# Transposes of a batch's cached keys: eight blocks in one step of the instruction order instead of four, and other pauses between steps

## Chip, cores and metric

The kernel runs on one core of a Trainium2 chip (trn2). The metric is the device time of one execution in microseconds. Three runs of the kernel before stand beside one profiled execution.

## What is computed

One step of a hybrid decoder layer for 256 prompt tokens and 32 sample tokens (8 batches of 4). Each sample batch has 256 cached keys and values, in two pages of a paged cache. The part that matters here is the attention of the sample tokens over the cached keys, in two branches: `x = 0` is stick-breaking attention, `x = 1` is block-sparse softmax attention, which with 256 cached keys comes to plain softmax over all of them.

```python
h = jnp.einsum('btd,de->bte', rms_norm(x, g), w_in)          # q, k, v of both branches, two gates
past_sbk = cache_sb_k[layer, page_table].reshape(dec_b, past_len, N_HEADS_SB, HEAD_DIM)
o_sb = stick_breaking(q_sb, jnp.concatenate([past_sbk, k_sb], axis=1),
                      jnp.concatenate([past_sbv, v_sb], axis=1), pos_s, k_pos_s)
m = sigmoid(gate_sb) * (o_sb @ w_proj_sb) + sigmoid(gate_mb) * (o_mb @ w_proj_moba)
x = x + m @ w_out
x = x + HierMoE(RMSNorm(x))
```

(The last three lines are shortened to their meaning.) The outputs are the normed results and the new keys and values.

## The kernel before

The work goes through four stages. First the input projection: 40 blocks of 128 output columns, each 24 matmuls of 128 x 288 (weights split into a high and a low part, `held`, lines 342 to 353; the tiles are called `g`). Into this dense stream the attention of the prompt and of the samples is woven. Then the two branch projections (tiles `p`), the output projection (tiles `o`), and last the experts, whose 50 MB of weights stream through a ring of buffers.

The order of TensorE's instructions is written by the kernel itself: line 136 puts PE under manual order, so PE gets its instructions as the Python code emits them. The class `Driver` (lines 78 to 119) decides that. It keeps a virtual clock `now` in nanoseconds. A stream (a generator such as `prompt_attn`, line 539, or `sample_attn`, line 601) emits a step and yields two numbers, a cost and a pause: the cost is added to `now`, and the stream is not asked again until the pause has also passed. While no stream is due, the dense stream emits its next pair of matmuls (cost 247). These numbers set the order alone; they are not times of the chip. The order on the other engines is made by a list scheduler when the program is built, so it can change when PE's order changes.

`sample_attn` works on groups `G` of four batches. For each batch it gathers the cached keys of one branch into a tile `kp` (POOL's indirect DMA, `pages`, line 593, into one of five buffers with the tag `pg`), and then for each half `c` of the keys it transposes four 128 x 128 blocks on PE (line 616) into a PSUM tile `pk`, which ScalarE or VectorE copies into `KT` (line 617). After four batches come 32 score matmuls into `ss` (line 622), the softmax or its stick-breaking counterpart, the transposes `pas` (line 634), the value product `pos` (lines 643 and 647), a masked copy `om` (line 650) and a last product `pd` (line 655).

PSUM tiles come from a pool with tags (line 142): `at` has four buffers. Every transpose of attention takes one of the four (`pk`, `pas`, `pa`, `ntr`, `ntv`, `rt`), and so do the prompt's scores (`sc`, two at a time, lines 545 to 561), `pos` and `pd`. A buffer is free again when its last reader is done. For the scores of branch 0 that is the subtraction in `soft_sb` (line 520), after three activations on ScalarE (513 to 515) and on VectorE the sum (517) and the scan (518). For the scores of branch 1 it is the second exponential (line 531). `pad` (lines 491 and 498) is the VectorE product that takes a finished `g` out of PSUM; the transposes `ntr` and `ntv` (line 414) read it. `rt` (line 459) transposes rotated heads.

Of the kernel before, what the change touches and what calls it, by code (L numbers as in the profile page):

```python
# [121 lines left out]
def build(tc, I, O):  # L122
# [21 lines left out]
    def P(tag, name):  # L144
        return ps.tile([128, 512], F32, tag=tag, name=name, bufs=NBUF[tag])
# [15 lines left out]
    def cc(name):  # L161
        a, b = AT[name]
        return blob[:, a:b]
# [233 lines left out]
    def start_sample(x):  # L397

        if S[x]["left"] or (x == 1 and "through" not in S[0]):
            return  # L400
        Qb = at.tile([128, 4, NB, NH, NQ], F32, tag="Qb", name=f"Qb{x}")
        nc.gpsimd.memset(Qb, 0.0)
        for j in range(4):
            for s in range(2):
                nc.gpsimd.tensor_copy(Qb[64 * s:64 * s + 64, j, :, 2 * j + s, :],
                                      S[x]["qT"][64 * s:64 * s + 64, j, 256:NT].rearrange("p (b q) -> p b q", q=NQ))
        S[x]["Qb"] = Qb
        drv.spawn(sample_attn(x), (3904.0, 3300.0)[x])
# [101 lines left out]
    def soft_sb(sc, w, resets, name):  # L510

        t = at.tile([128, 384], F32, tag="t1", name=f"t1{name}", bufs=2)
        nc.scalar.activation(t[:, :w], sc, AF.Abs)
        nc.scalar.activation(t[:, :w], t[:, :w], AF.Exp, scale=-1.0)
        nc.scalar.activation(t[:, :w], t[:, :w], AF.Ln, bias=1.0)
        s = at.tile([128, 384], F32, tag="t2", name=f"t2{name}", bufs=5)
        V.scalar_tensor_tensor(s[:, :w], sc, 0.0, t[:, :w], op0=ALU.max, op1=ALU.add)
        V.tensor_tensor_scan(out=t[:, :w][:, ::-1], data0=resets[:, ::-1], data1=s[:, :w][:, ::-1],
                             initial=0.0, op0=ALU.mult, op1=ALU.add)
        V.tensor_sub(s[:, :w], sc, t[:, :w])  # L520
        nc.scalar.activation(s[:, :w], s[:, :w], AF.Exp)
        return s
# [3 lines left out]
    def soft_mx(sc, segs, name):  # L526
        s = at.tile([128, 384], F32, tag="t2", name=f"p{name}", bufs=5)
        m = at.tile([128, 4], F32, tag="m", name=f"m{name}", bufs=4)
        for i, (a, b) in enumerate(segs):
            V.tensor_reduce(m[:, i:i + 1], sc[:, a:b], axis=AX.X, op=ALU.max, negate=True)  # L530
            last_exp[name[0] == "s"] = nc.scalar.activation(s[:, a:b], sc[:, a:b], AF.Exp, bias=m[:, i:i + 1],
                                                            accum_out=m[:, 2 + i:3 + i])
        ns = len(segs)
        V.reciprocal(m[:, 2:2 + ns], m[:, 2:2 + ns])
        for i, (a, b) in enumerate(segs):
            V.tensor_scalar_mul(s[:, a:b], s[:, a:b], m[:, 2 + i:3 + i])
        return s
# [55 lines left out]
    def pages(src, b, name):  # L593

        t = at.tile([128, 1024], F32, tag="pg", name=name, bufs=5)
        nc.gpsimd.indirect_dma_start(out=t, out_offset=None, in_=src,
                                     in_offset=bass.IndirectOffsetOnAxis(ap=pidx[:, b:b + 1], axis=0),
                                     bounds_check=NPHYS * PAGE // 2 - 1, oob_is_err=False)
        return t.rearrange("p (c d) -> p c d", c=2)

    def sample_attn(x):
        ck, cv = (I["cache_sb_k"], I["cache_sb_v"]) if x == 0 else (I["cache_moba_k"], I["cache_moba_v"])
        kT, vn, Qb = S[x]["kT"], S[x]["vn"], S[x]["Qb"]
        for G in range(2):
            pt = P("ss", f"ss{x}{G}")
            KT = []
            for bb in range(4):
                b = 4 * G + bb
                kp = pages(ck, b, f"kp{x}{b}")
                kt = at.tile([128, 1040], F32, tag="KT", name=f"KT{x}{b}", bufs=4).rearrange("p (j t) -> p j t", j=4)  # L610
                nc.gpsimd.tensor_copy(kt[:, :, 256:260], kT[:, :, 256 + 4 * b:260 + 4 * b])
                for c in range(2):
                    pk = P("at", f"pk{x}{b}{c}")
                    pv = pk.rearrange("p (j t) -> p j t", j=4)
                    for j in range(4):
                        nc.tensor.transpose(pv[:, j, :], kp[:, c, j * 128:(j + 1) * 128], ident)  # L616
                    nc.any.tensor_copy(kt[:, :, c:256:2], pv)  # L617
                    yield 440.0, (1051.0, 438.0)[x]
                KT.append(kt)
            for j in range(4):  # L620
                for bb in range(4):
                    mm(pt[32 * bb:32 * bb + 32, 0:260], Qb[:, j, 4 * G + bb, :, :].rearrange("p h q -> p (h q)"),  # L622
                       KT[bb][:, j, :], start=(j == 0), stop=(j == 3))
            mm(pt[:, 256:260], identb, newmask[x], start=False, stop=True, skip_group_check=True)
            yield 1900.0, 0.0
            if x == 0:
                a = soft_sb(pt[:, 0:260], 260, ones[:, 0:260], f"s{x}{G}")
                yield 0.0, 5569.0
            else:
                a = soft_mx(pt, [(0, 260)], f"s{x}{G}")  # L630
                yield 0.0, 5768.0
            pa = P("at", f"pas{x}{G}")
            for c in range(2):
                nc.tensor.transpose(pa[:, c * 128:(c + 1) * 128], a[:, c:256:2], ident)
            own = at.tile([128, 8, 4], F32, tag="own", name=f"own{x}{G}", bufs=2)
            V.tensor_mul(own, a[:, None, 256:260].broadcast_to([128, 8, 4]), cc(f"own{G}")[:, :, None].broadcast_to([128, 8, 4]))
            nc.tensor.transpose(pa[0:32, 256:384], own.rearrange("p b c -> p (b c)"), ident)
            aT = a
            nc.any.tensor_copy(aT[:, 0:256], pa[:, 0:256])
            nc.any.tensor_copy(aT[0:32, 256:384], pa[0:32, 256:384])  # L640
            yield 330.0, (3564.0, 1623.0)[x]
            po = P("at", f"pos{x}{G}")
            mm(po, aT[0:32, 256:384], vn[0:32, 2, :], start=True, stop=False)
            vps = [pages(cv, 4 * G + bb, f"vp{x}{G}{bb}") for bb in range(4)]
            for c in range(2):
                for bb in range(4):
                    mm(po[32 * bb:32 * bb + 32, :], aT[:, c * 128 + 32 * bb:c * 128 + 32 * bb + 32], vps[bb][:, c, :],  # L647
                       start=False, stop=(c == 1))
            om = at.tile([128, 512], F32, tag="om", name=f"om{x}{G}")
            V.tensor_mul(om.rearrange("p (h d) -> p h d", d=HD), po.rearrange("p (h d) -> p h d", d=HD),  # L650
                         cc("mask8")[:, :, None].broadcast_to([128, 8, HD]))
            yield 2700.0, 3712.0
            pd = P("at", f"pd{x}{G}")
            for j in range(4):
                mm(pd[:, j * 16:(j + 1) * 16], om[:, j * 128:(j + 1) * 128], cc("sel"), start=True, stop=True)
            nc.any.tensor_copy(oT[x][:, :, 256 + 16 * G:272 + 16 * G],
                               pd[:, 0:64].rearrange("p (j t) -> p j t", j=4))
            yield 430.0, 0.0
        if x == 0:
            S[0]["through"] = True  # L660
            start_sample(1)
# [705 lines left out]
```

## Time and profile before

| what | value |
|---|---|
| median of three runs | 415.95 us |
| lowest and highest run | 412.25 us, 420.18 us |
| the profiled execution | 413.99 us |
| its span, first to last instruction | 412.2 us |
| TensorE busy | 393.2 us of the span (95%) |
| mean granted TensorE clock | 0.989 |

Around the span of the profiled execution lie 413.99 - 412.2 = 1.8 us. PE is TensorE, DVE VectorE, ACT ScalarE, POOL GpSimd, SP the engine that issues most DMAs. Matmuls are pipelined, so the row of one is longer than the distance to the next start; the distance of starts is what one costs. A number in brackets behind a row is the idle time before it and what ended it.

### The profile page before, as it was taken

The page shows a single profiled execution, that of the slowest core. Times are in us where ns is not written, and L with a number is a line of the kernel's source. Part 1 is how long each engine was busy: PE and PEld are TensorE (multiplying, and loading weights), DVE is VectorE, ACT ScalarE, POOL GpSimd, SP SyncE. Part 2 cuts the span into 40 slices and gives each one's busy share as a digit, 9 for nine tenths or more (in the row PEclk, how much of TensorE's full clock was granted, in tenths as well). Part 3 has the DMA queues.
Part 4 walks back from the last instruction along what each step waited for, and adds up shares of the span by engine and source line. Part 5 has one row for each costly group of instructions (what it writes and reads, how often), then busy time and mean ns, then how long its engine had stood idle before and what let it go on. Part 6 is the DMA issues. An engine that isn't in the chain of part 4 may idle for free.

```text
span 412.2 us, 7107 instructions
## 1 busy us (share of the span) xinstructions
PE 393.2 (95%) x2706; PEld 293.5 (71%) x2706; DVE 207.9 (50%) x435; ACT 179.6 (44%) x349; POOL 94.3 (23%) x127
## 2 busy tenths in 40 slices
PE   7899999999999999999999999998999999999990
PEld 4799988858987977997999999984543333333350
DVE  3964468556543647134647785244540111126874
ACT  4854358577653664674554446232001111112353
POOL 3730222105343320610000232331002222033011
PEclk9999999999999999999999999999899999999997
DMA  8998636635743963663899999939599999999903
GB/s 263 327 355 277 222 103 230 223 118 205 260 158 91 338 235 103 220 240 103 192 381 395 341 324 389 409 88 303 189 313 413 410 416 412 417 414 410 343 32 122
DMA packets 56777, 111.12 MB, mean 270 GB/s; under 512 B 7621, under 2 KB 36941, under 8 KB 54689
## 3 DMA queue, kind: packets, MB, share of 16 engines
q1 hardware_dynamic: 49312, 86.56, 59.6%
q0 software_dynamic: 7120, 23.95, 15.8%
q8 instruction: 23, 0.38, 0.4%
q10 hardware_dynamic: 304, 0.09, 0.1%
q14 instruction: 18, 0.14, 0.1%
HBM read 104.72 MB, written 7.43 MB: 272 GB/s over the span
## 4 chain that ended last, share of the span: by engine, by line
PE 69%; DMA 20%; ACT 3%; issue 2%; DVE 2%; POOL 1%; SPq 1%; DVEq 0%; POOLq 0%
DMA w<-in_w_expert_up 15%; PE g L347 10%; PE g L351 10%; PE g L348 10%; DMA w<-in_w_expert_down 6%; PE gu L1154 4%; PE pk L616 3%; PE p L347 2%; PE p L348 2%; PE p L351 2%; PE ss L622 2%; PE o L347 2%; PE pos L647 2%; PE pd L1202 2%; PE po L588 2%
## 5 line engine op out<-in xcount | busy, mean ns | idle before, releaser
L347 PE MATMUL g<-xTh,hi 128*128 128x288 f32 x312 | 90.7, 311 | 0.0
L348 PE MATMUL g<-xTl,hi 128*128 128x288 f32 x312 | 85.7, 296 | 0.0
L1154 PE MATMUL gu<-w,xeT 128*64 128x512 f32 x256 | 62.0, 612 | 1.1 <-DMA w<-in_w_expert_up 0.7
L347 PEld LDWEIGHTS g<-xTh,hi 128*128 128x128 f32 x312 | 58.7, 188 | 1.0 <-issue 0.9
L348 PEld LDWEIGHTS g<-xTl,hi 128*128 128x128 f32 x312 | 58.9, 189 | 0.0
L351 PE MATMUL g<-xTh,li 128*128 128x288 f32 x312 | 50.5, 300 | 0.0
L333 DVE TENSOR_TENSOR li<-rawi,hi 128x1024 fp32r<-128x1024 f32 x39 | 47.3, 1215 | 3.0 <-ACT hi L328 3.0
L328 ACT CAST hi<-rawi 128x1024 fp32r<-128x1024 f32 x39 | 40.8, 1049 | 15.2 <-PE g L348 15.1
L351 PEld LDWEIGHTS g<-xTh,li 128*128 128x128 f32 x312 | 43.8, 189 | 1.7 <-issue 1.7
L1154 PEld LDWEIGHTS gu<-w,xeT 128*64 128x64 f32 x256 | 18.7, 139 | 33.1 <-issue 31.4
L1202 PE MATMUL pd<-w,hT 128*64 128x512 f32 x128 | 29.2, 598 | 0.0
L993 DVE TENSOR_TENSOR xeT<-xe,gpk 128x512 f32<-128x512 f32 x16 | 10.4, 686 | 22.9 <-PE xe L991 22.9
L617 ACT COPY KT<-pk 128x512 f32<-128x512 f32 x30 | 18.6, 639 | 7.1 <-PE pk L616 6.7
L1172 DVE SCALAR_TENSOR_TENSOR h<-gu,rsl,h 128x256 f32<-128x256 f32 x8 | 3.9, 484 | 34.3 <-ACT h L1169 34.3
L973 POOL DMA_INDIRECT xe<-x_d,inv x7 | 7.3, 1041 | 56.7 <-DVE rsl L1141 26.2
L1169 ACT ACTIVATE h<-gu,rsl 128x256 f32<-128x256 f32 x8 | 3.8, 474 | 37.5 <-PE gu L1154 19.8
L1202 PEld LDWEIGHTS pd<-w,hT 128*64 128x64 f32 x128 | 8.6, 136 | 15.4 <-issue 13.7
L616 PE MATMUL pk<-blob,kp 128*128 128x128 f32 x128 | 19.4, 274 | 0.1
L505 DVE TENSOR_TENSOR gate<-g,rb 128x288 f32<-128x288 f32 x16 | 7.3, 457 | 21.3 <-PE g L351 21.1
L347 PE MATMUL p<-oTh,hp 128*128 128x288 f32 x64 | 17.5, 296 | 0.0
L348 PE MATMUL p<-oTl,hp 128*128 128x288 f32 x64 | 17.4, 294 | 0.0
L1212 ACT COPY y<-pd 128x512 f32<-128x512 f32 x10 | 5.9, 586 | 23.6 <-PE pd L1202 23.6
(301 smaller groups left out, 708.6 us busy)
## 6 DMA issues: line engine op xcount, KB each, us to landing
rawi<-in_w_in SPq DMA_DIRECT2D x19, 1024.0 KB
w<-in_w_expert_gate SPq DMA_DIRECT2D x32, 512.0 KB
w<-in_w_expert_up SPq DMA_DIRECT2D x32, 512.0 KB
w<-in_w_expert_down SPq DMA_DIRECT2D x16, 1024.0 KB
rawo<-in_w_out SPq DMA_DIRECT2D x4, 1024.0 KB
y_d<-y POOLq DMA_DIRECT2D x10, 256.0 KB, 9.6
rawp<-in_w_proj_sb SPq DMA_DIRECT2D x2, 1024.0 KB
rawp<-in_w_proj_moba SPq DMA_DIRECT2D x2, 1024.0 KB
```

The source lines that it names most:

```text
L328: nc.scalar.copy(h, src)
L333: V.tensor_sub(l, src, h.bitcast(F32))
L347: mm(o, h[:, k, :], mh[k], start=(k == 0), stop=False)
L348: mm(o, h[:, k, :], ml[k], start=False, stop=False)
L351: mm(o, l[:, k, :], mh[k], start=False, stop=(k == n - 1))
L588: mm(po[64 * s:64 * s + 64, 128 * c:256], vn[:, c, h * 64:(h + 1) * 64], aT[s][:, 256 * c:256 + 128 * c], start=(c == 0), stop=(c == 1))
L616: nc.tensor.transpose(pv[:, j, :], kp[:, c, j * 128:(j + 1) * 128], ident)
L617: nc.any.tensor_copy(kt[:, :, c:256:2], pv)
L622: mm(pt[32 * bb:32 * bb + 32, 0:260], Qb[:, j, 4 * G + bb, :, :].rearrange("p h q -> p (h q)"), KT[bb][:, j, :], start=(j == 0), stop=(j = ...
L993: i = V.tensor_mul(xeT[:, ks, :], pv, gpk[:, ks, None].broadcast_to([128, 4, 128]))
L1154: mm(pt[64 * i:64 * i + 64, :], xeTs[pr][:, k, 64 * i:64 * i + 64], W[pr, k // 4, i][:, :, k % 4, :], start=(k == 0), stop=(k == 7))
L1202: mm(pd[64 * i:64 * i + 64, :], hT[:, k, 64 * i:64 * i + 64], W[pr, 2, i][:, k, c * 512:(c + 1) * 512], start=(k == 0), stop=(k == 1))
```

## The change

The yield moves out of the loop over the halves of the keys. A step is now both halves of a batch's keys, eight blocks into two PSUM tiles one after the other. The cost of a step is 880 instead of twice 440. The pause is 1800 (branch 0) or 1100 (branch 1) behind eight blocks, where it was 1051 or 438 behind four.

```diff
                     for j in range(4):
                         nc.tensor.transpose(pv[:, j, :], kp[:, c, j * 128:(j + 1) * 128], ident)
                     nc.any.tensor_copy(kt[:, :, c:256:2], pv)
-                    yield 440.0, (1051.0, 438.0)[x]
+                yield 880.0, (1800.0, 1100.0)[x]
                 KT.append(kt)
```

A batch took 2 x (440 + 1051) = 2982 of the virtual clock in branch 0 and takes 880 + 1800 = 2680; in branch 1 it took 1756 and takes 1980. The number of instructions on every engine is the same.

TensorE in branch 0, first group of batches, around the transposes of the third and fourth batch's keys. `pk` are the key transposes, `g` the dense blocks, `ntr` and `rt` transposes of the other branch's new heads; a number behind a name is a buffer's own. Before:

```order
L348 MATMUL g_836<-xTl,hi_832 128x288
L616 MATMUL pk_839<-blob,kp_809 128x128 x4
L347 MATMUL g_836<-xTh,hi_832 128x288
L348 MATMUL g_836<-xTl,hi_832 128x288
L414 MATMUL ntr_847<-blob,pad_113 128x128 x3
L459 MATMUL rt_861<-blob,nr_755 128x128 x3
L347 MATMUL g_836<-xTh,hi_832 128x288
L348 MATMUL g_836<-xTl,hi_832 128x288
L616 MATMUL pk_874<-blob,kp_868 128x128 x4
```

The same transposes `ntr` of `pad_113` in the changed kernel:

```order
L348 MATMUL g_860<-xTl,hi_856 128x288
L414 MATMUL ntr_867<-blob,pad_113 128x128 x3
L459 MATMUL rt_881<-blob,nr_787 128x128 x3
L616 MATMUL pk_892<-blob,kp_886 128x128 x4
L616 MATMUL pk_898<-blob,kp_886 128x128 x4
L347 MATMUL g_860<-xTh,hi_856 128x288
```

Where four groups of transposes in a row of the order were parted by two dense matmuls each, `ntr`, `rt` and both halves of a batch's keys now follow each other.

VectorE at the product `pad_113` that `ntr` reads. `t_765` to `t_788` belong to the second pair of prompt scores. Before:

```order
L617 COPY KT_731<-pk_793 128x4x128
L517 SCALAR_TENSOR_TENSOR t_779<-sc_765,t_775 128x384
L518 SCALAR_TENSOR_TENSOR t_775<-rst_99,t_779 128x384
L498 TENSOR_TENSOR pad_113<-g_744,rb 128x288
L333 TENSOR_TENSOR li_1002<-rawi_998,hi_1000 128x1024
L520 TENSOR_TENSOR t_779<-sc_765,t_775 128x384
L517 SCALAR_TENSOR_TENSOR t_788<-sc_766,t_784 128x384
```

And in the changed kernel:

```order
L517 SCALAR_TENSOR_TENSOR t_769<-sc_755,t_765 128x384
L517 SCALAR_TENSOR_TENSOR t_778<-sc_756,t_774 128x384
L518 SCALAR_TENSOR_TENSOR t_765<-rst_99,t_769 128x384
L518 SCALAR_TENSOR_TENSOR t_774<-rst_99,t_778 128x384
L498 TENSOR_TENSOR pad_113<-g_750,rb 128x288
L333 TENSOR_TENSOR li_1002<-rawi_998,hi_1000 128x1024
L520 TENSOR_TENSOR t_769<-sc_755,t_765 128x384
```

The product stood behind one sum and one scan; now both sums and both scans of the pair stand ahead of it.

TensorE in branch 0 after the first group's scores: `pa` are the transposes of two prompt heads' weights, `pos` the product with cached values. Before:

```order
L555 MATMUL sc_1071<-bfc 128x128
L351 MATMUL g_1004<-xTh,li_1002 128x288 x2
L579 MATMUL pa_1100<-blob,t_779 128x128 x3
L579 MATMUL pa_1105<-blob,t_788 128x128 x3
L459 MATMUL rt_1110<-blob,nr_1018 128x128 x3
```

And in the changed kernel:

```order
L647 MATMUL pos_1098<-vp_1112,t2s_941 32x512
L579 MATMUL pa_1126<-blob,t_769 128x128 x3
L579 MATMUL pa_1131<-blob,t_778 128x128 x3
L459 MATMUL rt_1136<-blob,nr_1015 128x128 x3
L351 MATMUL g_1004<-xTh,li_1002 128x288 x2
```

The value product moved ahead of the two transposes `pa`; it stood some rows behind them.

## Rows read from the trace of the kernel before

**Rows 1.** Page, busy time by engine, and the chain that ended last

```profile
PE 393.2 (95%) x2706; PEld 293.5 (71%) x2706; DVE 207.9 (50%) x435; ACT 179.6 (44%) x349; POOL 94.3 (23%) x127
PE 69%; DMA 20%; ACT 3%; issue 2%; DVE 2%; POOL 1%; SPq 1%; DVEq 0%; POOLq 0%
```

**Rows 2.** Windows: us; busy PE, PEld, DVE, ACT, POOL; clock; DMA share; GB/s

```profile
50.00:100.00 50.00, 47.64 (x390) 39.95 (x389) 32.27 (x65) 33.61 (x68) 11.34 (x16) 1.00 0.52 176
100.00:150.00 50.00, 50.00 (x436) 43.60 (x436) 25.26 (x60) 29.05 (x64) 18.45 (x25) 1.00 0.66 223
150.00:200.00 50.00, 50.00 (x408) 41.92 (x401) 22.53 (x50) 28.16 (x62) 9.24 (x16) 1.00 0.51 168
...
267.00:277.00 10.00, 10.00 (x85) 9.71 (x84) 3.05 (x17) 2.91 (x9) 4.09 (x6) 1.00 0.28 99
...
287.00:297.00 10.00, 8.79 (x38) 4.14 (x37) 6.03 (x18) 0.00 (x0) 2.07 (x2) 0.83 0.54 185
```

**Rows 3.** Timeline of PE, 58 to 74 us: start, duration, engine, line, operation

```profile
58.50 0.60 PE L616 MATMUL pk<-blob,kp 128*128 128x128 f32 x4
58.86 0.38 PE L347 MATMUL g<-xTh,hi 128*128 128x288 f32 x1
59.07 0.29 PE L348 MATMUL g<-xTl,hi 128*128 128x288 f32 x1
59.20 0.30 PE L347 MATMUL g<-xTh,hi 128*128 128x288 f32 x1
...
61.13 0.92 PE L552 MATMUL sc<-kT,qT 64*128 64x128 f32 x6 [0.15 <-ACT nr L445]
...
62.46 0.66 PE L616 MATMUL pk<-blob,kp 128*128 128x128 f32 x4
...
67.45 0.52 PE L414 MATMUL ntr<-blob,pad 128*128 128x128 f32 x3 [0.54 <-DVE t L518]
...
74.11 0.49 PE L459 MATMUL rt<-blob,nr 128*128 128x128 f32 x3
```

**Rows 4.** Timeline of ACT, 59 to 68 us

```profile
59.14 0.63 ACT L617 COPY KT<-pk 128x512 f32<-128x512 f32 x1
...
62.44 0.53 ACT L521 ACTIVATE t<-t 128x384 f32<-128x384 f32 x1 [1.36 <-DVE t L520]
...
64.03 0.94 ACT L514 ACTIVATE t<-t 128x384 f32<-128x384 f32 x2
64.85 0.52 ACT L515 ACTIVATE t<-t 128x384 f32<-128x384 f32 x1
...
66.63 1.13 ACT L617 COPY KT<-pk 128x512 f32<-128x512 f32 x2
```

**Rows 5.** Timeline of DVE, 61 to 93 us

```profile
61.85 1.01 DVE L520 TENSOR_TENSOR t<-sc,t 128x384 f32<-128x384 f32 x2
...
66.00 0.96 DVE L518 TENSOR_TENSOR_SCAN t<-rst,t 128x384 f32<-128x384 f32 x1
66.87 0.43 DVE L498 TENSOR_TENSOR pad<-g,rb 128x288 f32<-128x288 f32 x1
...
88.47 1.02 DVE L517 SCALAR_TENSOR_TENSOR t<-sc,t 128x384 f32<-128x384 f32 x2 [0.88 <-ACT t L515]
89.41 0.95 DVE L518 TENSOR_TENSOR_SCAN t<-rst,t 128x384 f32<-128x384 f32 x1
...
92.80 0.69 DVE L650 TENSOR_TENSOR om<-pos,blob 128x512 f32<-128x512 f32 x1
```

**Rows 6.** Timeline of PE, 85 to 99 us

```profile
85.80 0.81 PE L579 MATMUL pa<-blob,t 128*128 128x128 f32 x6
87.27 0.55 PE L459 MATMUL rt<-blob,nr 128*128 128x128 f32 x3 [0.66 <-ACT t L581]
...
98.97 0.55 PE L414 MATMUL ntr<-blob,pad 128*128 128x128 f32 x3 [0.81 <-ACT oT L656]
```

**Rows 7.** Timeline of POOL, gather of keys for the second group

```profile
92.91 1.02 POOL L596 DMA_INDIRECT kp<-in_cache_sb_k,pidx  x1 [14.66 <-PE pos L647]
```

## Prediction

> **What bounds the kernel now.** I read the page first, then the stretches, then the timelines of PE, ACT and DVE around the transposes that move. TensorE is busy for 95% of the span, and it makes 69% of the chain that ended last [rows 1]. In the stretch with the cached keys (50 to 200 us) PE has no idle time to speak of but 2.4 us between 50 and 100 us, DVE and ACT are busy for about half of the time, and the DMA queues too [rows 2]. So what an edit is worth here is read on PE alone: the sum of its instructions' costs, which this change leaves, and the waits of an engine that takes its instructions in order. DMA does bind later, among the experts, but between 267 and 277 us its share falls to 0.28 [rows 2]: the transfers have run ahead there and stand still until PE goes on. So I take a delay of PE ahead of that point to reach the end at full price, though part of it may be lost in that slack.
>
> Three waits can be seen in the stretch, and all hang on the four PSUM buffers `at`. At 67.45 the transposes `ntr` wait for VectorE, which has a scan (518) and then the product `pad` ahead [rows 3, 5]. At 87.27 `rt` waits for ScalarE's copy of `pa` (581), and at 98.97 `ntr` waits for ScalarE's copy of `pd` (656) [rows 6]. The key transposes at 62.46 start behind the subtraction (520) that frees a buffer of the prompt's scores: it starts at 61.85, two of them take 1.01, and the first is over at about 62.36 [rows 3, 5].
>
> **The change part by part.** *Fewer alternations.* Four key transposes start at 58.50, the dense block follows at 58.86, its second matmul 0.21 us later, and from there on the distance is 0.13 [rows 3]. So four transposes between dense blocks cost 0.36 and 0.08, that is 0.44 us, or 0.11 each.  Eight in a row are then 0.88 us, the same as twice four. The 16 joined steps save nothing by themselves; the bounds I keep are -1.3 (all 16 save the 0.08) and 0.
>
> *Moved waits.* Here I walk through the new order with the durations of the rows, on the clock of the trace before. "Late" means PE stands.
>
> Place A, branch 0, first group (from 58.50). Both halves of the first batch's keys are done at 59.4, four dense matmuls at 60.0. The prompt's second scores then need the two buffers the keys just filled. ScalarE's first copy starts at 59.14 and takes 0.63 [rows 4]; a second one starts 0.57 later (1.13 for two), so it ends at about 60.35: 0.4 late. The scores take 1.07, to 61.5. All four buffers are now scores, so `ntr` stands until the first subtraction ends at 62.4: 0.9 late. Then `ntr` (0.33), keys (0.44), 0.15 for the copy of `ntr`, keys again: 63.95. Twelve dense matmuls, four, eight key transposes, four and six more bring PE to 68.45, where it meets `ntr` of `pad_113`. ScalarE starts at 62.44 with two exponentials and two activations 513 (1.6, as 62.44 to 64.03), then 514, a key copy, 514, a key copy (0.41 + 0.57 + 0.41 + 0.57) and two of 515 (0.41 apart): the first 515 ends at about 66.5, the second at 66.9 [rows 4]. VectorE does both sums from 66.55 (0.47 each), both scans (0.87 from start to start, the time from 66.00 to 66.87) and `pad` (0.43): ready at 69.7 [rows 5]. So 1.3 late, where before the `pad` stood behind one sum and one scan. Behind it `ntr` and `rt` fill the two free buffers, the next keys wait for the copy of `ntr`: 0.4 late. The fourth batch's keys are done at 71.7. Before, they were done at 74.11 [rows 3], with 26 dense matmuls (3.47) and one `ntr` (0.33) more behind them, that is 70.3 for the same work. Place A costs 1.4 us.
>
> Place B, branch 0, after the first group's scores. The value product now precedes `pa`. It holds one buffer until `om`, the scores hold two until 520, so both `pa` go through the last one: the second waits for the first one's copy (0.33 and about 0.35 behind the start: 0.65 late), and `rt` waits for `om`, which on VectorE stands behind two sums and one scan (from about 89.2: 0.94, 0.87, then `om` 0.69, to 91.7 [rows 5]) while PE is there at 91.0: 0.7 late. The 1.35 stand against the wait at 87.27 before: `pa` takes 0.66 of work from 85.80, so it was 0.8 [rows 6]. Place B costs 0.55.
>
> Place C, the second group's first keys. `pd` is copied by VectorE now, both halves follow without a wait, and `ntr` comes later: the wait of 0.81 before 98.97 [rows 6], 1.0 with the tail of the matmul ahead, goes. What is late next is `rt` behind the second batch's keys, which asks for a buffer of the scores and gets it when 520 ends. On my clock those scores end at 96.6 and the first 515 at 98.95; behind it VectorE has a sum, a scan, a sum, a `pad` and 520 (0.47 + 0.87 + 0.47 + 0.43 + 0.5 [rows 5]), to 101.75, and PE is there at 101.3: 0.5 late. Place C gains 0.5.
>
> Place D, branch 1. Two dense matmul groups between key halves go, and the scores of the second pair need the buffers of the first, free after the second exponential: about 0.2 late. The fourth batch's second copy ends just as the 32 score matmuls reach it: 0.15. PE was not idle from 100 to 200 us before [rows 2], so nothing can be gained here but hidden tails. I take 0.35, with -0.3 and 1.0 as the ends (the upper end being one wait of place A's size).
>
> *The gathers.* Each half uses the same tile `kp`, so no key is needed before its transposes' step. The second group's second batch is issued at 92.91 [rows 7] and in my walk is first read at about 100.5; a step is 0.3 us shorter in the order, so I cost it at nothing. If that cover failed, the keys would be late by the excess of a gather over 7.6 us, and the three behind it with them.
>
> The sum: 1.4 + 0.55 - 0.5 + 0.35 = 1.8 us slower. On the profiled execution that is 413.99 + 1.8 = 415.8 us. That execution lies 2 us under the median of the runs; the median plus 1.8 would be 417.7. I take 417.0, between the two and nearer to the median.
>
> **The rivals.** *R1, the waits go.* With all that was late in the trace before gone (idle 0.15, 0.54, 0.66 and 0.81 in brackets [rows 3, 6], and some 0.25 of a matmul's tail ahead of each, as at 98.97 and 87.27: 3.2 us) the kernel takes 413.99 - 3.2 = 410.8. For it: longer pauses give the copies time, and place C does lose its wait. Against it: at place A four buffers are scores in either order.
>
> *R2, nothing moves.* Waits change places and cancel: 414 to 416. For it: VectorE and ScalarE have half of their time free [rows 2], so a wait that I count twice may be one. Against it: the scans that stand ahead of `pad` are a fact of the order.
>
> *R3, every pair waits (the slower side).* Place: each of the 16 steps. A step now takes two of four `at` buffers at once, so its second half could always stand behind a copy. Price: at the size of the wait at 98.97, 0.81 us each, 13 us, so 427. It decides from 0.52 us a step on, where 16 steps make 8.3 us. Against it: in my walk the second half itself is late by no more than 0.2, because ScalarE copies in 0.57 and there is dense work ahead of most steps.
>
> *R4, the clock.* Granted clock is 1.00 from 50 to 200 us, though PE stood for 2.4 us, and 0.83 between 287 and 297 us, after PE stood for 1.2 of ten [rows 2]. If the waits and the longer runs of transposes brought that 0.83 into the four stretches of key transposes, each as long as the first (58.50 to 74.11 [rows 3], 15.6 us, 62 in all), they would take 62 x (1/0.83 - 1) = 12.7 us more: 413.99 + 1.8 + 12.7 = 428.5. Against it: at place A PE stood for longer than anywhere in the stretch before and the clock stayed at its upper level, 2.4 GHz. The Trainium skill ("TensorE: Matmul & The Clock Gate", Part 4: PE-mode transpose) says that transposes do not count as PE activity in the way that matmuls do, and its section "A second HAM failure mode: psum-queue depth-cycling" tells of a kernel whose clock swings since PE halts briefly for PSUM buffers. By that rule this change, which lengthens runs of transposes and adds such halts, is a risk. The trace of before speaks against it, with 1.00 in the stretches that hold all 128 key transposes [rows 2].
>
> **How the numbers follow.** A measurement of this kernel can tell about 2% (8.3 us) from no change; the three runs alone spread over 8 us. Chances: my forecast 0.44, R2 0.25, R1 0.20, R3 0.07, R4 0.04. The forecast, R1 and R2 lie within 2%. Slower by over 2% is R3 and most of R4, less what of R3 stops short of it: 0.08. Faster by over 2% would need more than twice the waits that exist, and only the spread of the runs could show it: 0.03. Within 2%: 0.89. The range goes from R1 (410.8, about 411.5 with the runs' median above the profile) to the forecast with the upper ends of place D (1.0 for 0.35) and a doubled place A (1.4), 417.7 + 2.1, and 3 us for the spread of a median: 423. Outside stay R3, R4 and the far side of R1.
>
> **What would show it.** Right: idle of PE between 50 and 100 us above the 2.4 of before; `ntr` near 68 us waiting over a microsecond for VectorE with both scans ahead of `pad`; the second `pa` and `rt` after the value product waiting one behind the other; no wait of `ntr` at the second group's first keys; granted clock 1.00 up to 267 us. Wrong: key transposes themselves as the waiting row in most of 16 steps (R3), a clock below 1.00 there (R4), or PE without idle time between 50 and 200 us (R1). If PE loses its 1.8 us but the end does not move, the step that a delay reaches the end at full price has failed.

## The result, and the profile of the changed kernel

The changed kernel takes 417.56 us (median of 20 executions, 413.87 to 420.33), the kernel before 415.29 us in the same set (20 executions): ratio 1.007, 95% interval 1.0048 to 1.0092. In a second set (experiment 5) the ratio was 1.0045 (1.001 to 1.0079). These ratios leave out executions that took over 1.5% longer than the fastest of the same kernel. The changed kernel is slower by 0.5 to 0.7 per cent, less than the 2% that a measurement tells from no change with ease. The profiled execution of the changed kernel took 415.58 us with a span of 413.7.

Two lines of the page, busy time by engine and the chain that ended last, answer to [rows 1]:

```profile
PE 393.6 (95%) x2706; PEld 292.3 (71%) x2706; DVE 207.7 (50%) x435; ACT 178.8 (43%) x349; POOL 94.5 (23%) x127
PE 68%; DMA 18%; DVE 5%; ACT 3%; issue 2%; POOL 1%; DVEq 0%; SPq 0%; POOLq 0%; ACTq 0%
```

No engine's work has changed; the chain has 5% of VectorE where it had 2%. The windows of the changed kernel (columns as in [rows 2]):

```profile
50.00:100.00 50.00, 47.15 (x384) 39.20 (x384) 29.56 (x62) 32.76 (x68) 13.86 (x17) 1.00 0.51 168
100.00:150.00 50.00, 49.31 (x422) 42.84 (x424) 27.24 (x65) 28.53 (x62) 16.13 (x24) 1.00 0.67 228
150.00:200.00 50.00, 49.97 (x415) 40.76 (x408) 21.89 (x48) 27.70 (x62) 9.46 (x16) 1.00 0.49 161
267.00:277.00 10.00, 10.00 (x82) 9.73 (x81) 1.70 (x4) 1.69 (x5) 4.16 (x6) 1.00 0.33 132
```

PE stands for 2.85 us between 50 and 100 us (2.36 before) and for 0.69 between 100 and 150 (0.00 before); from 150 to 200 us there is no difference, and the clock is 1.00 in all of it. Where it stands is in the view of the waits of PE, here from 50 to 218 us (who waits, for whom; us in total, times, longest):

```profile
PE ntr L414 <- DVE pad L498: 1.0, 1, 1.0
PE ntr L414 <- DVE t L520: 0.9, 1, 0.9
PE pa L579 <- ACT t L581: 0.6, 1, 0.6
PE pas L637 <- DVE own L636: 0.5, 1, 0.5
PE pk L616 <- ACT nr L445: 0.2, 1, 0.2
PE rt L459 <- DVE t L520: 0.2, 1, 0.2
```

Before, four rows of this kind stood there: 0.15, 0.54, 0.66 and 0.81 [rows 3, 6]. Now the timeline of PE where they lie, with the rows that answer to [rows 3, 6], and the first matmul of the projection `p`:

```profile
58.30 1.04 PE L616 MATMUL pk<-blob,kp 128*128 128x128 f32 x8
59.09 0.38 PE L347 MATMUL g<-xTh,hi 128*128 128x288 f32 x1
59.31 0.30 PE L348 MATMUL g<-xTl,hi 128*128 128x288 f32 x1
...
62.26 0.55 PE L414 MATMUL ntr<-blob,pad 128*128 128x128 f32 x3 [0.89 <-DVE t L520]
...
69.46 0.52 PE L414 MATMUL ntr<-blob,pad 128*128 128x128 f32 x3 [0.98 <-DVE pad L498]
...
70.55 1.09 PE L616 MATMUL pk<-blob,kp 128*128 128x128 f32 x8 [0.24 <-ACT nr L445]
71.39 0.38 PE L347 MATMUL g<-xTh,hi 128*128 128x288 f32 x1
...
89.51 0.55 PE L579 MATMUL pa<-blob,t 128*128 128x128 f32 x3
90.62 0.55 PE L579 MATMUL pa<-blob,t 128*128 128x128 f32 x3 [0.57 <-ACT t L581]
91.26 0.55 PE L459 MATMUL rt<-blob,nr 128*128 128x128 f32 x3
...
97.08 1.12 PE L616 MATMUL pk<-blob,kp 128*128 128x128 f32 x8
...
101.39 0.55 PE L459 MATMUL rt<-blob,nr 128*128 128x128 f32 x3 [0.19 <-DVE t L520]
...
119.55 0.28 PE L637 MATMUL pas<-blob,own 128*32 128x128 f32 x1 [0.50 <-DVE own L636]
...
218.14 0.30 PE L347 MATMUL p<-oTh,hp 128*128 128x288 f32 x1
```

The last of these rows in the trace of before:

```profile
216.44 0.30 PE L347 MATMUL p<-oTh,hp 128*128 128x288 f32 x1
```

And the timeline of DVE that the waits hang on, which answers to [rows 5]: at 67 us the two scans ahead of `pad`, at 90 us `om` between the two scans, at 97 us the copy of `pd`, at 118 us a product of 1.22 us ahead of `own`:

```profile
66.22 1.02 DVE L517 SCALAR_TENSOR_TENSOR t<-sc,t 128x384 f32<-128x384 f32 x2 [2.00 <-ACT t L515]
67.16 1.80 DVE L518 TENSOR_TENSOR_SCAN t<-rst,t 128x384 f32<-128x384 f32 x2
68.88 0.43 DVE L498 TENSOR_TENSOR pad<-g,rb 128x288 f32<-128x288 f32 x1
...
88.73 1.02 DVE L517 SCALAR_TENSOR_TENSOR t<-sc,t 128x384 f32<-128x384 f32 x2 [6.30 <-ACT t L515]
89.67 0.95 DVE L518 TENSOR_TENSOR_SCAN t<-rst,t 128x384 f32<-128x384 f32 x1
90.54 0.67 DVE L650 TENSOR_TENSOR om<-pos,blob 128x512 f32<-128x512 f32 x1
91.12 0.95 DVE L518 TENSOR_TENSOR_SCAN t<-rst,t 128x384 f32<-128x384 f32 x1
...
97.27 0.23 DVE L656 COPY oT<-pd 128x64 f32<-128x64 f32 x1 [1.79 <-PE pd L655]
...
118.17 1.22 DVE L333 TENSOR_TENSOR li<-rawi,hi 128x1024 fp32r<-128x1024 f32 x1
119.30 0.19 DVE L636 TENSOR_TENSOR own<-t2s,blob 128x32 f32<-128x32 f32 x1
```

**Two numbers for each kernel.** From the start of the first key transposes to the start of the first matmul of the projection `p` (L347), PE has the same work in every kernel of this study (1280 instructions of the same kinds), so this time shows what its waits cost. It was 216.44 - 58.50 = 157.9 us before and 218.14 - 58.30 = 159.8 after: 1.9 us lost. From there to the end of the span it was 195.8 and 195.6. These two, taken from the timelines and the spans, and the granted clock in the windows between 270 and 300 us, stand in this table for all profiled executions, with the ratio of each kernel to the kernel before in its own set:

| kernel | to `p`, us | `p` to end, us | clock under 1.00 in windows of 10 us, 270 to 300 | ratio (95%) |
|---|---|---|---|---|
| before | 157.9 | 195.8 | 0.83 | 1 |
| changed | 159.8 | 195.6 | 0.83 | 1.007 (1.0048 to 1.0092) |
| 1, branch 0 alone | 159.8 | 198.6 | 0.86, 0.79 | 1.0071 (1.0037 to 1.0105) |
| 2, branch 1 alone | 158.1 | 193.8 | none | 1.002 (0.9983 to 1.0057) |
| 3, joined, old pauses | 161.8 | 196.3 | 0.83 | 1.0199 (1.0156 to 1.0241) |
| 4, apart, new pauses | 158.3 | 193.6 | none | 1.0016 (0.9984 to 1.0048) |
| 5, changed again | 159.9 | 197.3 | 0.86, 0.80 | 1.0045 (1.001 to 1.0079) |
| 6, scan behind `pad` | 159.0 | 193.7 | none | 1.0019 (0.9996 to 1.0041) |
| 7, as 3, copy on DVE | 160.3 | 196.9 | 0.89, 0.77 | 1.0068 (1.003 to 1.0106) |
| 8, before, copy on DVE | 160.1 | 197.6 | 0.89, 0.77 | 1.0063 (1.0031 to 1.0095) |
| 9, first batch apart | 159.4 | 195.2 | 0.83 | 1.0098 (1.006 to 1.0136) |
| 10, before, repaired | 156.7 | 194.0 | none | 1.0002 (0.9957 to 1.0048) |
| 11, as 10, again | 156.6 | 198.5 | 0.83, 0.83 | 0.9991 (0.9953 to 1.003) |
| 12, as 10, `rt` later | 156.6 | 198.2 | 0.75, 0.74 | 0.9992 (0.9955 to 1.003) |

The ratios also carry the granted clock, which differs from execution to execution. An estimate at equal clock can be worked out from all executions of an experiment and of the kernel before in its set: a straight line of time against mean granted clock, with one constant for the changed code. The constants are 2.0 us (experiment 1), 0.4 (2), 0.8 (4), 2.1 (5), 1.1 (6), 2.3 (7) and 2.6 (9), and for the repaired kernels about -0.5 (10), -0.2 (11) and 0.1 (12), each with a standard error of 0.2 to 0.3. Experiments 3 (3.3, error 0.5) and 8 (0.9) lose time by a lower clock too, which such a constant leaves out.

### The profile page after: what moved, and what is told of

Same layout as the page of the kernel before. It is cut to its first block, busy times and chain, and to the rows that moved or that the text cites. A ratio compares the mean times of both kernels' runs of the same rounds, so it can differ in the third digit from the quotient of the medians.

```text
span 413.7 us, 7106 instructions
## 1 busy us (share of the span) xinstructions
PE 393.6 (95%) x2706; PEld 292.3 (71%) x2706; DVE 207.7 (50%) x435; ACT 178.8 (43%) x349; POOL 94.5 (23%) x127
## 4 chain that ended last, share of the span: by engine, by line
PE 68%; DMA 18%; DVE 5%; ACT 3%; issue 2%; POOL 1%; DVEq 0%; SPq 0%; POOLq 0%; ACTq 0%
DMA w<-in_w_expert_up 15%; PE g L347 10%; PE g L351 9%; PE g L348 9%; DMA w<-in_w_expert_down 4%; PE gu L1154 4%; PE pk L616 2%; PE p L347 2%; PE p L348 2%; PE p L351 2%; PE o L347 2%; PE xe L982 2%; PE ss L622 2%; PE pd L1202 2%; PE po L588 2%
## 5 line engine op out<-in xcount | busy, mean ns | idle before, releaser
L347 PE MATMUL g<-xTh,hi 128*128 128x288 f32 x312 | 89.1, 307 | 0.0
L1154 PE MATMUL gu<-w,xeT 128*64 128x512 f32 x256 | 60.3, 598 | 1.2 <-DMA w<-in_w_expert_up 0.9
L347 PEld LDWEIGHTS g<-xTh,hi 128*128 128x128 f32 x312 | 58.7, 188 | 1.6 <-issue 1.6
L347 PE MATMUL p<-oTh,hp 128*128 128x288 f32 x64 | 17.5, 296 | 0.0
L616 PE MATMUL pk<-blob,kp 128*128 128x128 f32 x128 | 17.0, 275 | 0.3 <-ACT nr L445 0.2
```

The lines of the kernel that those rows point to most:

```text
L347: mm(o, h[:, k, :], mh[k], start=(k == 0), stop=False)
L1154: mm(pt[64 * i:64 * i + 64, :], xeTs[pr][:, k, 64 * i:64 * i + 64], W[pr, k // 4, i][:, :, k % 4, :], start=(k == 0), stop=(k == 7))
```

## The experiments

**1 and 2: which branch.** The diff of each against the changed kernel, first branch 0 alone, then branch 1 alone:

```diff
-                yield 880.0, (1800.0, 1100.0)[x]
+                    if x == 1:
+                        yield 440.0, 438.0
+                if x == 0:
+                    yield 880.0, 1800.0
```

```diff
-                yield 880.0, (1800.0, 1100.0)[x]
+                    if x == 0:
+                        yield 440.0, 1051.0
+                if x == 1:
+                    yield 880.0, 1100.0
```

Expected of the first:

> The joined step with its new pause in branch 0 alone; branch 1 keeps two halves and the old pause. Theory T1 (the cost is waits of TensorE at single places of branch 0: ntr behind the first subtraction and behind the product pad, the second pa, and the product own): the whole loss is here, 1.9 us of PE up to the first matmul of the gated projection p (216.44 us before, 218.14 after), PE waits for pad 1.0, for 520 0.9, pa 0.6, own 0.5 as in the changed kernel, ratio to the kernel before about 1.005 to 1.007. Rival T2 (each of the 16 joined pairs pays 0.1 to 0.2 us for its buffers, in both branches alike): half of the loss, ratio about 1.0035, and 0.9 us of PE.

Expected of the second:

> The joined step with its new pause in branch 1 alone; branch 0 as before. Theory T1 (all of the loss is waits in branch 0): ratio 1.000 (0.999 to 1.001), the waits of before at 67, 87 and 99 us stand again, and no new one between 140 and 200 us. Rival T2 (each joined pair pays alike): ratio about 1.0035, 0.9 us more PE between 140 and 200 us. My forecast on record had 0.35 us here, that is 1.0008.

Branch 0 alone has the six waits of the changed kernel, to 0.1 us, its 159.8 us to `p`, and its ratio; branch 1 alone has the waits of before and 158.1 us. So the loss is in branch 0, and the eight joined steps of branch 1 cost 0.2 us together. T2, a price per joined pair, falls.

**3 and 4: joining or the pause.** Experiment 3 joins the halves and gives a batch the time of two old pauses; experiment 4 leaves them apart with half the new time each:

```diff
-                yield 880.0, (1800.0, 1100.0)[x]
+                yield 880.0, (2102.0, 876.0)[x]
```

```diff
-                yield 880.0, (1800.0, 1100.0)[x]
+                    yield 440.0, (900.0, 550.0)[x]
```

> The steps joined, but with the time of two old pauses (2102 and 876) behind each, so that a batch takes as long in the order as before. In this order pad of the third key projection stands on DVE ahead of the second sum and of both scans. Theory T1 (what costs is where the new pauses put ntr, pad and own among the scans): ntr near 68 us waits for pad by less than 0.3 us where the changed kernel has 0.98, the wait of ntr for the subtraction 520 near 62 us (0.9) stays, since both pairs of key buffers stand ahead of the second scores here too; ratio to the kernel before 1.000 to 1.004. Rival T3 (joining alone is the cost, whatever the pause): ratio 1.006 or more, and waits in front of the key transposes.

> The halves stay apart as before, with half of the new time each (900 and 550): the pause alone. Theory T1 (place by place): the second scores come ahead of the second pair of halves, so the wait of ntr for 520 near 62 us goes back to under 0.2; pad stands on DVE behind one scan, so ntr waits for it by about 0.5 as before (1.0 after); ratio to the kernel before 0.998 to 1.002. Rival T3 (joining is the cost): also 1.000. Rival T4 (the longer pause alone is the cost): 1.006 or more.

Experiment 4 came out as T1 had it in time, 158.3 us to `p` and a ratio of 1.0016, though its longest wait is one of 0.7 us for the copy of `pd`, and none is left for `pad`. Experiment 3 is a miss: 1.0199 where T1 had at most 1.004. That is 8.2 us, of which the profiled execution shows 3.9 on PE up to `p` (161.8). Its waits of PE, 50 to 218 us:

```profile
PE pk L616 <- ACT oT L656: 2.4, 1, 2.4
PE ntr L414 <- DVE t L520: 0.9, 1, 0.9
PE rt L459 <- ACT t L581: 0.7, 1, 0.7
PE pos L643 <- ACT ps L640: 0.3, 1, 0.3
```

The wait for `pad` is gone and the 0.9 for 520 stays, as expected; but at the second group's first keys the second half waits 2.4 us for ScalarE's copy of `pd`, which stands behind a cast of 1.04 us and the activations of the scores. And the clock falls behind that wait, as the windows of experiment 3 show (columns as in [rows 2]):

```profile
90.00:100.00 10.00, 7.63 (x65) 5.81 (x58) 4.28 (x10) 6.19 (x14) 4.21 (x5) 0.97 0.82 266
100.00:110.00 10.00, 10.00 (x72) 9.98 (x72) 7.57 (x19) 5.31 (x10) 3.25 (x3) 0.85 0.40 120
```

T3 had the size (1.006 or more), but its reason, a cost of joining wherever it is done, does not fit: the greatest part of what PE loses up to `p` is one wait at one of 16 steps. Experiment 7 takes that wait away.

**5: the changed kernel again**, for the granted clock of each execution.

> The changed kernel once more, beside the kernel before on the same chip, for the granted clock of each execution. Theory T1 (waits of TensorE alone): the six waits of the changed kernel return at the same places within 0.1 us, the mean clock over its runs is that of the kernel before (0.989), ratio 1.004. Theory T5 (the waits also bring the granted clock down in some executions, as in the 10 us behind the wait of 2.4 us of the kernel with joined steps and old pauses): the mean clock is lower by 0.002 to 0.004, ratio 1.006 to 1.009.

The six waits return to the tenth of a microsecond, with 159.9 us to `p`. Ratio 1.0045, 1.9 us of 414.3, which is what PE loses, and 2.1 us at equal clock: T1's waits alone account for the loss. The mean granted clock over all twelve executions is 0.9866, and 0.9883 for the kernel before on the same chip, 0.0017 lower, where T5 had 0.002 to 0.004. So T5 is not needed for the loss, but that these waits never lower the clock in any execution is not shown.

**6: one scan behind `pad`.** The order on PE stays, row for row:

```diff
-            V.tensor_mul(t[:, 0:NT], o, rb)
+            i = V.tensor_mul(t[:, 0:NT], o, rb)
+            if j == 1 and not isq:
+                with tc.issue_after(i.ins):
+                    scans.pop()()
...
+        if name == "03":
+            scans.append(rest)
+        else:
+            rest()
```

(Shortened; `rest` is the scan, the subtraction and the exponential of `soft_sb`. The added lines move those in this file down, so that 520 is 524 in the rows below, 579 is 590 and 636 is 647.)

> The changed kernel with one scan on DVE, that of the second head of the second pair, put behind pad of the third key projection; the order on PE is the same row for row. If the 1.0 us that ntr waits near 69 us is due to that scan, as place A of the forecast has it, the wait falls to 0.0 to 0.3, the first matmul of the projection p comes 0.7 to 1.0 us earlier against the first key transposes than in the changed kernel, and the ratio to the kernel before goes from 1.007 to about 1.005. If the wait is set by something else (the product's own input, a matmul's tail), it stays at 0.7 or more.

The row of `pad` is gone from the waits of PE, the other five stand:

```profile
PE ntr L414 <- DVE t L524: 0.9, 1, 0.9
PE pa L590 <- ACT t L592: 0.6, 1, 0.6
PE pas L648 <- DVE own L647: 0.5, 1, 0.5
PE pk L627 <- ACT nr L445: 0.2, 1, 0.2
PE rt L459 <- DVE t L524: 0.2, 1, 0.2
```

159.0 us to `p`, 0.8 less than the changed kernel: that wait was set by the second scan on DVE. The ratio goes from 1.0045 to 1.0019 on the same chip; the two intervals overlap, but at equal clock the loss falls from 2.1 to 1.1 us, so the price of the wait reaches the end.

**7 and 8: the copy of the first `pd` on VectorE**, in the kernel of experiment 3 and in the kernel before, with PE's order unchanged:

```diff
-            nc.any.tensor_copy(oT[x][:, :, 256 + 16 * G:272 + 16 * G],
+            (V if (x, G) == (0, 0) else nc.any).tensor_copy(oT[x][:, :, 256 + 16 * G:272 + 16 * G],
```

> The kernel with joined steps and the old pauses, whose second key transposes waited 2.4 us for ScalarE's copy of pd, with that one copy on VectorE; the order on PE is the same row for row. Theory T1 (each loss is one wait at one place): the 2.4 us go, less than 0.5 us for VectorE in their place, the granted clock between 100 and 110 us is 1.00 instead of 0.85, and the ratio falls from 1.020 to 1.003 to 1.008. Rival T3 (joining with these pauses is slow by itself): the ratio stays at 1.015 or more.

> The kernel before with the copy of the first pd on VectorE instead of ScalarE; the order on PE is the same row for row. If the wait of 0.8 us at 98.97 hangs on ScalarE's copy, it goes with about 0.2 us of a matmul's tail: PE 1.0 us less up to the first matmul of p, ratio 0.997. If it hangs on pd itself or on something that VectorE would meet too, the wait stays and the ratio is 1.000.

In experiment 7 the 2.4 us become 0.8 where under 0.5 was expected (and 0.5 at a later pair), the clock stays at 1.00 between 100 and 110 us, and 1.0199 becomes 1.0068, as T1 had it. Up to `p` the two profiled executions differ by 1.5 us (161.8 and 160.3): so much are that wait and the clock behind it worth there. The two ratios, from different sets, differ by 5.4 us. The executions of experiment 3 have a mean clock of 0.977, those of experiment 7 one of 0.983; where the clock fell in those that were not profiled, no trace shows. Of what is left to experiment 7, 0.9 us is the wait for 520 that the changed kernel has too.

Experiment 8 is a miss in the other direction. The order on DVE puts the copy behind a scan, a product of 1.20 us, a sum and a subtraction, to 100.90 us, and `ntr` now takes the buffer of the key transposes and waits longer. The first row of its waits, and its window behind it:

```profile
PE ntr L414 <- ACT KT L617: 1.5, 1, 1.5
```

```profile
100.00:110.00 10.00, 10.00 (x70) 9.98 (x70) 5.61 (x17) 5.64 (x10) 2.25 (x2) 0.83 0.49 155
```

So the same edit takes a wait of 2.4 us away in one order and makes one of 0.8 into 1.5 in another. Of the twelve executions of this kernel ten have a mean clock of 0.976 to 0.981, two 0.993 and 0.994.

**9: only the first batch apart.**

```diff
+                    if (x, G, bb) == (0, 0, 0):
+                        yield 440.0, 1051.0
+                if not ((x, G, bb) == (0, 0, 0)):
+                    yield 880.0, (1800.0, 1100.0)[x]
```

> The changed kernel, but the very first key batch of branch 0 in two halves with the old pause; the other 15 batches joined. Theory T1 (the waits of the first group come from that one pair, which fills the buffers ahead of the second scores): the wait of ntr for 520 near 62 us and the second scan ahead of pad go, and ntr waits for pad by about 0.5 near 67 us as in the kernel before. But in this order pd stands five matmuls behind the scores and right ahead of the second group's first key pair, as in the kernel with old pauses, so the same wait of 2.4 us for ScalarE's copy of pd is to come back near 98 us, and with it (theory T5) a granted clock below 1.00 between 100 and 110 us: ratio 1.008 to 1.014. Rival T2 (each joined pair pays): ratio 1.0065, no wait over 1.1 us.

The first half of the expectation held: no wait for 520 near 62 us, and `ntr` waits 0.5 for `pad` (at 100.75, however, not near 67, where none is left). So that one pair makes both waits of the first group. The wait for `pd` came back, but with 1.1 us (the cast on ScalarE runs 1 us earlier than in experiment 3), and the clock stayed at 1.00. The ratio of 1.0098 is in T1's range for a reason that T1 did not give: PE loses 1.4 us to `p` in the profiled execution, and the ratio says 4. At equal clock it is 2.6. What the other executions do there, no trace shows.

Taken together: the wait for 520 stands where the first pair is joined (the changed kernel, experiments 1 and 3) and not where its halves are apart (before, 2, 4 and 9). The second scan ahead of `pad` needs the joined pair and the new pause together, since 3, 4 and 9 do not have it.

**10, 11 and 12: the kernel before with its waits repaired.** The scan behind `pad` as in experiment 6 (name "02"), and

```diff
-        yield 330.0, 5271.0
+        yield 330.0, 5271.0 + (600.0 if (j, isq) == (3, 0) else 0.0)
```

with 1000 for 600 in experiment 12; experiment 11 is the kernel of experiment 10 once more. (This edit, too, moves the lines down by up to ten.)

> The kernel before with its own waits repaired: the scan that stands ahead of pad of the third key projection put behind it, and the transposes rt of the fourth projection 0.6 us later in the order, which puts two matmuls ahead of them at 87 us and six ahead of ntr at 99 us. Theory T1 (a wait of PE is lost at full price, and so is its removal won): ntr near 67 us waits 0.0 to 0.2 instead of 0.5, rt near 87 us 0.0 to 0.4 instead of 0.7, ntr near 99 us 0.0 to 0.2 instead of 0.8; from the first key transposes to the first matmul of p 156.0 to 156.9 us instead of 157.9; ratio to the kernel before 0.994 to 0.998. Rival T6 (what is taken from one place turns up at the next): the waits return elsewhere, ratio 0.999 to 1.002.

> The repaired kernel before once more, since its interval (0.9957 to 1.0048) holds both the gain that its trace shows on PE (1.3 us, ratio 0.997) and none. Theory T1 (the gain reaches the end): ratio 0.994 to 0.999 in this set too, 156.7 us from the first key transposes to the first matmul of p. Rival T6 (the gain is given back behind p, in the experts): ratio 0.999 to 1.004 again, and from p to the end more than 194 us where no stretch of the trace has a clock below 1.00.

> As the repaired kernel, with the transposes rt of the fourth projection 1.0 us later in the order instead of 0.6, which puts four matmuls ahead of them at 87 us instead of two; the other places of the order on PE stay. Theory T1: the 0.4 us that rt still waits go to 0.2 or less, 156.3 to 156.6 us from the first key transposes to the first matmul of p, ratio 0.993 to 0.998. Rival T6: a wait of the same size at the next instruction (ntr or po), ratio 0.999 to 1.004.

All three have 156.6 or 156.7 us to `p`, 1.3 less than before; the 0.4 us that experiment 12 takes from `rt` win nothing, since `ntr` behind it then waits 0.2 where it did not. What is left of the waits in experiment 10:

```profile
PE rt L459 <- ACT t L591: 0.4, 1, 0.4
PE ntr L414 <- ACT KT L627: 0.4, 1, 0.4
PE sc L562 <- ACT nr L445: 0.2, 1, 0.2
```

But the ratios are 1.0002, 0.9991 and 0.9992, each with an interval that holds both 0.997 (the gain in full) and 1. T1's ranges (0.994 to 0.998, 0.994 to 0.999, 0.993 to 0.998) were missed by all three centres, and at equal clock (-0.5, -0.2 and 0.1 us) most of the 1.3 us does not reach the end; where it goes, these runs do not show. The one execution of them with no lowered clock between 270 and 300 us has 194.0 us from `p` to the end, the longest of the four such executions in the table, but only by 0.2 to 0.4 us. A version that is measurably faster than both kernels was not found.

## Why the prediction was right, and where its steps were not

The forecast of 417.0 us (411.5 to 423.0) stands beside 417.56 measured, and its term of 1.8 us beside 1.9 lost on PE up to `p`. That the two times lie 0.6 us apart is in part luck: the forecast went by three runs of the kernel before with a median of 415.95, twenty put it at 415.29, and the medians of the two kernels differ by 2.3 us. The step of 1.8 us is the one to judge. By its own steps, each wait being the bracket and 0.16 us of tail (the last matmul's row goes on for 0.27 us where the next start would follow in 0.11):

- *Joined transposes save nothing: right.* Eight start at 58.30, the dense block at 59.09, its second matmul 0.22 later: 0.79 and 0.09, the 0.88 of the forecast.
- *Place A, 1.4 us: right in sum.* The fourth batch's keys are done at 71.39, 13.1 us behind the start of the first, where the forecast had 71.7 - 58.5 = 13.2; so the place costs 1.3. With the tail, `ntr` behind 520 waits 1.05 (0.9 forecast), `ntr` behind `pad` 1.14 (1.3 forecast), and the next keys 0.40 (0.4). The sums began at 66.22 and not 66.55 and `pad` was over at 69.3 and not 69.7, but 0.2 of each is only that this trace starts its first key transposes 0.2 us earlier. One step did not come: the second scores, forecast 0.4 late behind the copies of the keys, show no wait, so a part of the agreement is luck. (The terms that the forecast lists from 62.4 on add up to 63.8 and not to 63.95; that would make `ntr` 1.5 late behind `pad` and leave the 71.7.) Experiments 6 and 9 show the two causes, the second scan and the first joined pair.
- *Place B, 0.55 us: too much.* The second `pa` waits 0.57 and its tail, as forecast, but `rt` starts 0.64 behind it, of which 0.33 are the transposes: 0.3 late instead of 0.7. The order on VectorE was as forecast, two sums and one scan ahead of `om`; the step that failed is its start. The sums began at 88.73 and not 89.2, so `om` was over at 91.21 and not 91.7. With the tail that is 1.0 against the 0.8 of before, so the place costs 0.2.
- *Place C, a gain of 0.5 us: right, 0.6 in size.* The wait of 0.81 [rows 6] is gone; `rt` waits 0.19 and a tail for 520 at 101.39, where 0.5 was forecast.
- *Place D, branch 1, 0.35 us: smaller.* Experiment 2 gives 0.2 for all of it.
- *A place that the forecast did not have:* `pas` at 119.55 waits 0.50 for `own`, since in the new order a `pad` and a `li` (1.22 us) stand ahead of `own` on DVE. It is worth about 0.6 us and makes up for B and D. The forecast walked the second group's keys, and not its `own`. That the 1.8 us came out although this place was missing is luck. Places B and C and this one are read from the traces; no experiment took their waits away one by one.
- *The gathers at nothing: right.* No key transposes wait for a DMA; the second group's second gather is issued at 89.83, 3 us earlier than in [rows 7], since the value product frees its tiles earlier.
- *A delay of PE reaches the end at full price: right for delays.* With no lowered clock between 270 and 300 us, the rest takes 193.6 to 194.0 us, whether `p` starts at 214.75 or at 218.53, and at equal clock experiments 1 and 5 lose 2.0 and 2.1 us at the end, with 1.9 and 2.0 on PE up to `p`. For a gain it is not shown (experiments 10 to 12).

Of the rivals, R1 (the waits go) is out by the interval of the ratio, R2 (they cancel) by the 1.9 us that PE loses up to `p` in three executions (the changed kernel twice, and experiment 1), and R3 (every pair waits) by experiments 1 and 2. R4 did not come in this kernel, its clock being 1.00 from 50 to 200 us. But longer waits in the same stretch show its mechanism: behind waits of PE of 1.0 us and less (the changed kernel) and of 1.1 (experiment 9) the clock stayed at its upper level of 2.4 GHz, and waits of 1.5 and 2.4 (experiments 8 and 3) were followed by 0.83 and 0.85 in the window of 100 to 110 us. This is one execution of each of these experiments, and at the start of the experts the clock fell behind waits of 0.8 and 0.9 us as well, so the size of one wait alone does not decide. The price can be read row for row against the kernel with the same order on PE whose clock stayed at 1.00: behind the wait PE loses another 1.6 us in experiment 8 (against the kernel before) and about 1.0 in experiment 3 (against experiment 7, up to the last of the `ntr` at 102.70). The Trainium skill ("TensorE: Matmul & The Clock Gate", "A second HAM failure mode: psum-queue depth-cycling") tells of a kernel whose clock swings because PE halts briefly and often between groups of matmuls while it cycles through PSUM banks. The runs here show falls behind single longer halts for such buffers, and none in this stretch behind the few short ones of this change.

## What to carry to other kernels

When a change moves work in a hand-made order, its price is not in the instructions that it groups but in the few places where an in-order engine then meets a buffer not yet free: walk each of them with the durations of the rows, and go on to the end of the moved stretch, since one place was missed here. Ask for each wait which instruction stands ahead of the releaser on its own engine: here one scan of 0.87 us in the wrong place was nearly the whole wait, and it could be moved without touching the order of the waiting engine. An edit that shortens a wait in one order can make a longer one in another (experiments 7 and 8), so it has to be read anew in each. And a wait removed is not yet time won: experiments 10 to 12 took 1.3 us off PE and show little of it at the end.

## What was not expected of the hardware

**The spread of the executions is the clock, in steps.** Of the 35 executions of the kernel before beside experiments 5 to 8, ten have a mean granted clock of 0.994 or 0.995 and take 412.7 us on average, sixteen have 0.986 to 0.992 and take 414.4, nine have 0.980 to 0.982 and take 416.1: steps of 1.7 us. In the table the same steps stand in the time from `p` to the end: 193.6 to 194.0 us with no window below 1.00 between 270 and 300 us, 195.2 to 196.3 with one at 0.83, and 196.9 to 198.6 with two. Ten us at 0.83 are 1.7 us of work less, too, though the sum of two such windows gives the step only roughly (experiment 12: 5.1 us missing, 4.4 longer than the mean of the four without). PE stands there while the experts begin (0.9 us for `rsl`, 0.8 for `OHs` in the waits of the kernel before), and whether the clock then falls differs from one execution to the next of the same kernel. Up to `p`, the two profiled executions of the changed kernel agree to 0.1 us, and so do those of the repaired one (experiments 10 and 11). So a difference of 2 us between two profiled executions of this kernel says nothing on its own, and the time up to `p` says much.

**The copy of `pd`.** In the kernel before, ScalarE is free from 97.29 us and `pd`'s last matmul ends, as modelled, at 97.68, yet the copy starts at 98.70; with the copy on a free VectorE in experiment 7 it starts 1.0 us behind `pd` too, and in the changed kernel at once. The profile puts the release down to the key transposes `pk` behind `pd` in the first two, whose last row ends 0.55 us before the copy in both (98.15 and 96.55), and to `pd` itself in the changed kernel. Why the copy waits for them was not settled.
